# A hybrid decoder layer on one core: side work placed by modelled clocks, and an inverse that turns its blocks through DRAM

## The chip, the core and the metric

The kernel runs on one core of a Trainium2 chip. Its five engines (TensorE for matmuls, VectorE, ScalarE, GpSimd, and SyncE, which issues most DMAs) run side by side, each through its own queue in order. The metric is the device time of one execution in microseconds; the output must be the reference's.

## The reference

One decoder layer for 512 positions and a model width of 2048, all in float32. After an RMSNorm, one projection feeds three mixers: differential attention (4 heads, causal, ALiBi), sliding-window attention (8 query heads, window 128, sinks) and an RWKV-7 time mixing of 16 heads of 64 channels. Their outputs are concatenated, projected and added to the input; then come an RMSNorm, a SwiGLU feed-forward part of width 5632, and a last RMSNorm.

```python
def step(S, inp):                      # RWKV-7, per head, S is 64 x 64
    r_t, w_t, k_t, v_t, a_t, b_t = inp
    sa = jnp.einsum('bhvk,bhk->bhv', S, a_t)
    S = S * w_t[:, :, None, :] + sa[..., None] * b_t[:, :, None, :] + v_t[..., None] * k_t[:, :, None, :]
    return S, jnp.einsum('bhvk,bhk->bhv', S, r_t)

kk = kk / jnp.maximum(jnp.sqrt(jnp.sum(kk * kk, axis=-1, keepdims=True)), 1e-12)
y = wkv7_scan(r4, hs(decay), k4, v4, -kk, kk * a4)
```

## The kernel before

**Wide matmuls.** Every weight matrix is cut into items (`proj`, `wout_items`, `ffn_items`), and an item is 24 or 48 matmuls of 128 x 128 weights against 512 columns: weights and activations are split into a high and a low part (`weights`, L154), and three of the four products are summed. `sequence` runs the items one after another; while item n runs, item n+1's weights are loaded by SyncE into one of three `raw` buffers, cast by ScalarE (L169) and subtracted by VectorE (L170).

**Side work.** The mixers' other steps are generators in lanes. `dense_k` calls `pump` after every fourth wide matmul, and `pump` lets each lane go one step, to its next `yield`; so the order of TensorE, which is kept as written, is made by counting matmuls. `wait(n)` lets a lane pass n turns. `need(name)` pumps, with no wide matmul between, until a lane has finished.

**RWKV, by pairs of heads.** For each of eight pairs (`pair_items`) there are three items, `k`, `r`, `v`. `rates` makes decays: sigmoids, and one scan (L437) for each of eight chunks of 64 positions. `prep` makes the chunk matrices: `bt` (transposes), the products `gr` of both heads, masked by VectorE (L549) into `linv`, `zl` and `gr`, and `vt` and `bon`. `inverse` inverts the 64 x 64 unit triangles of eight chunks and two heads: the diagonal 32 x 32 blocks are copied together (L594 to L596), transposed on VectorE (L600), eliminated in 30 steps of two VectorE operations (L608, L609), transposed back twice (L617 `xtt`, L618 `xnn`), and the off-diagonal block comes from two groups of 16 matmuls, `pt` and `po`. `chain` then goes through the eight chunks: `z`, a copy on ScalarE, `u`, a copy, `S`, an update on VectorE (L678), and outputs `y`. `post` normalizes; `spill` writes the result to DRAM (`mix`).

**Attention.** `diff_head` and `swa_tile` work in blocks of 128 queries: `scores` (matmuls `sa`, `sb` and the softmax on VectorE and ScalarE), `turned` (transposes `wt`, `wtb`) and `values` (`oa`, `ob`), each a step of its own. Then the output projection `po` runs in two halves and, from 1050 us on, the feed-forward part.

Of the kernel before, what the change touches and what calls it, by code (L numbers as in the profile page):

```python
# [14 lines left out]
P = 128  # L15
# [34 lines left out]
for _name, _w in (  # L50
    ("ident", 128), ("onesbd", 128), ("ones", 128), ("centre", 128), ("mask", 128),
    ("eps", 1), ("gneps", 1),
):
    CST[_name] = _n
    _n += _w
# [3 lines left out]
def constants():  # L59
# [15 lines left out]
    put("gneps", np.full((P, 1), GN_EPS, np.float32))  # L75
    return c
# [10 lines left out]
class Kernel:  # L87
    def __init__(self, tc, ins, out, dbg=None, stop=None):
# [6 lines left out]
        self.lanes = [[], [], [], [], [], [], []]  # L95
        self.order = [self.lanes[j] for j in (2, 6, 5, 0, 1, 3, 4)]
        self.done = set()
        self.flags = set()
        self.count = 0
        self.quantum = 4  # L100
        self.delay = 150
# [21 lines left out]
    def tr(self, out, src):  # L123
        self.tc.keep_in_program_order(self.nc.tensor.transpose(out, src, self.cst("ident", P)))  # L124

    def pump(self):
# [9 lines left out]
    def wait(self, n):  # L139
        for _ in range(-(-n * 4 // self.quantum)):  # L140
            yield

    def need(self, name):
        for _ in range(10000):
            if name in self.done:
                return
            self.pump()
# [28 lines left out]
    def dense_k(self, ps, wts, rhs, k, n, m=P, cols=slice(0, T)):  # L176
        (his, los), (xh, xl) = wts, (x[:, cols] for x in rhs[k])
        for i, (w, x) in enumerate(((his[k], xh), (his[k], xl), (los[k], xh))):
            self.mm(ps[:m, :], w, x, start=(k == 0 and i == 0), stop=(k == n - 1 and i == 2))
            self.count += 1  # L180
            if self.count % self.quantum == 0:
                self.pump()
# [26 lines left out]
    def run(self):  # L209
        nc, tc = self.nc, self.tc  # L210
        with contextlib.ExitStack() as es:
            enter = es.enter_context
            self.cp = enter(tc.tile_pool(name="cp", bufs=1))
# [126 lines left out]
    def mixer_items(self, enter):  # L340
# [11 lines left out]
        f = rp.tile([P, T], F32, tag="r", name="f_wl")  # L352
# [8 lines left out]
        for j in range(2):  # L361
            def go(ps, j=j):
                f = rp.tile([P, T], F32, tag="r", name=f"f_gl{j}")
# [13 lines left out]
        for t in self.linv:  # L377
            nc.gpsimd.memset(t, 0.0)
        self.mix = [None] * 16
# [6 lines left out]
    def pair_items(self, hp):  # L386
# [5 lines left out]
        for j, n in ((1, "k"), (0, "r"), (2, "v")):  # L392
            def go(ps, n=n):
                if hp:
                    self.need(f"{n}{hp - 1}")
                f = self.rp.tile([P, T], F32, tag=n, name=f"{n}{hp}")
# [15 lines left out]
    def rates(self, hp):  # L412
# [4 lines left out]
        if not hp:  # L417
            yield from self.wait(16)
# [3 lines left out]
        g2 = rp.tile([P, 2, P], F32, tag="g2", name=f"g2_{hp}", bufs=3)  # L422
        nc.sync.dma_start(out=w2, in_=self.i["w2"][:, ch])
        nc.sync.dma_start(out=a2, in_=self.i["a2"][:, ch])
        nc.sync.dma_start(out=g2, in_=self.i["g2"][:, :, ch])
        q["g2"] = g2
# [5 lines left out]
        yield  # L432
        self.sigmoid(sg[:, :, 1:65], ps.rearrange("p (n c) -> p n c", c=C))
        yield from self.wait(2)
        cum = rp.tile([P, NCH, 65], F32, tag="kk", name=f"cum{hp}")
        for n in range(NCH):
            nc.vector.tensor_tensor_scan(out=cum[:, n], data0=self.cst("ones", 65), data1=sg[:, n], initial=0.0,  # L437
                                         op0=ALU.mult, op1=ALU.add)
        yield
        yield  # L440
# [5 lines left out]
        yield  # L446

        ps = self.pm.tile([P, T], F32, tag="m", name=f"pa{hp}")
        self.mm(ps, a2, self.al[:96, :], start=True, stop=True)
        yield  # L450
        a = rp.tile([P, T], F32, tag="a", name=f"a{hp}")
        self.sigmoid(a, ps, nbias=self.na0[:, hp:hp + 1])
        q["D"] = rp.tile([P, NCH], F32, tag="D", name=f"D{hp}", bufs=3)
        nc.vector.tensor_tensor(out=q["D"][:, 0:NCH - 1], in0=W[:, 0:NCH - 1, 64], in1=V[:, 1:NCH, 0], op=ALU.mult)
        q.update(W=W, V=V, a=a)

    def prep(self, hp):
# [8 lines left out]
        kk_g = self.col("k_k", hp)  # L466
        yield
        nc.scalar.activation(rn, k, AF.Square, scale=kk_g)
        yield from self.wait(1)
# [3 lines left out]
        yield  # L473
        nc.vector.tensor_scalar(out=kk, in0=ps, scalar1=1e-24, scalar2=None, op0=ALU.max)
        yield
        nc.scalar.activation(kk, kk, AF.Ln)
        nc.scalar.activation(kk, kk, AF.Exp, scale=-0.5)
        yield from self.wait(2)
        nc.vector.scalar_tensor_tensor(out=kk, in0=k, scalar=kk_g, in1=kk, op0=ALU.mult, op1=ALU.mult)
        yield  # L480
# [757 lines left out]
```

## Time and profile before

| | us |
|---|---|
| median of three runs | 2511.62 (2507.73 to 2515.35) |
| profiled execution | 2510.84 |
| its span, first to last instruction | 2509.0 |
| TensorE busy | 2445.0 (97%) |
| VectorE busy | 1277.2 (51%) |
| ScalarE busy | 835.3 (33%) |

Matmuls are pipelined and their recorded durations overlap, so the distance of two starts tells more than a duration, and 97% busy is not 97% of what TensorE could do. A wait is the idle time before an instruction together with what ended it. The granted clock is the share of TensorE's full clock, 2.4 GHz, that the chip let through; 0.50 is its lower level, 1.2 GHz.

### The profile page before, as it was taken

How to read it: one execution, taken by the hardware profiler on the slowest of the kernel's cores; microseconds unless marked ns; L12 is line 12 of the kernel's file. 1: busy time of each engine (PE TensorE's matmuls, PEld its weight loads, DVE VectorE, ACT ScalarE, POOL GpSimd, SP SyncE). 2: the span in 40 equal slices, each digit the busy share in tenths (PEclk: the TensorE clock that was granted, in tenths of full speed). 3: DMA queues.
4: the chain of work that ended last, by engine and by line, in shares of the span. 5: the costliest groups of instructions: out<-in, count | busy, mean ns of one | idle time of the engine just before them, and what ended most of it. 6: DMA issues, size and time to landing. Idle time of an engine off the chain costs nothing.

```text
span 2509.0 us, 30180 instructions
## 1 busy us (share of the span) xinstructions
PE 2445.0 (97%) x12072; PEld 1932.7 (77%) x12072; DVE 1277.2 (51%) x2201; ACT 835.3 (33%) x1439; POOL 92.4 (4%) x115
## 2 busy tenths in 40 slices
PE   8989999999999999999999999999999999999997
PEld 6766666666767678888888888888888888888887
DVE  6777788877454534434343433333343434343437
ACT  5544455553444523322222222222222222212224
POOL 3000000000000001200000000000000000000006
PEclk9989899999999999999999999999999999999999
DMA  5211111111322423323232323232322223232324
GB/s 180 75 51 59 57 59 59 59 55 59 100 78 89 145 93 126 101 93 98 95 100 94 101 93 101 93 101 93 101 94 99 96 98 97 96 99 95 101 93 135
DMA packets 76142, 232.65 MB, mean 93 GB/s; under 512 B 8282, under 2 KB 17122, under 8 KB 76002
## 3 DMA queue, kind: packets, MB, share of 16 engines
q1 hardware_dynamic: 71106, 224.04, 27.5%
q10 hardware_dynamic: 4896, 6.69, 0.8%
q8 instruction: 95, 1.56, 0.3%
q14 instruction: 45, 0.37, 0.0%
HBM read 222.30 MB, written 8.39 MB: 92 GB/s over the span
## 4 chain that ended last, share of the span: by engine, by line
PE 69%; DVE 1%; ACT 1%; issue 0%; POOL 0%; DVEq 0%; ACTq 0%; POOLq 0%
PE pg L121 19%; PE pu L121 19%; PE pd L121 18%; PE po L121 7%; PE pd_qb L121 1%; PE pd_va L121 1%; PE pd_qa L121 1%; PE pd_ka L121 1%; PE sb L121 0%; PE oa L121 0%; PE ob L121 0%; POOL acc L1053 0%; PE wtb L124 0%; PE sa L121 0%; DVE y L1151 0%
## 5 line engine op out<-in xcount | busy, mean ns | idle before, releaser
L121 PE MATMUL pd<-al,wh_wd 128*128 128x512 f32 (+1 forms) x768 | 285.3, 371 | 0.5 <-DVE al L1088 0.5
L121 PE MATMUL pd<-ah,wh_wd 128*128 128x512 f32 (+1 forms) x768 | 285.4, 372 | 0.4 <-DVE y L1107 0.4
L121 PE MATMUL pd<-ah,wl_wd 128*128 128x512 f32 (+1 forms) x768 | 285.2, 371 | 0.0
L121 PE MATMUL pu<-x1h,wh_wu 128*128 128x512 f32 x704 | 274.3, 390 | 0.0
L121 PE MATMUL pu<-x1h,wl_wu 128*128 128x512 f32 x704 | 273.9, 389 | 0.0
L121 PE MATMUL pu<-x1l,wh_wu 128*128 128x512 f32 x704 | 273.9, 389 | 0.0
L121 PE MATMUL pg<-x1h,wl_wg 128*128 128x512 f32 x704 | 273.9, 389 | 0.0
L121 PE MATMUL pg<-x1h,wh_wg 128*128 128x512 f32 x704 | 273.9, 389 | 0.0
L121 PE MATMUL pg<-x1l,wh_wg 128*128 128x512 f32 x704 | 273.9, 389 | 0.0
L1107 DVE TENSOR_TENSOR y<-y,pd 128x512 f32<-128x512 f32 (+1 forms) x192 | 122.7, 642 | 207.6 <-PE pd L121 207.4
L169 ACT CAST wh_wd<-raw_wd 128x1024 fp32r<-128x1024 f32 x96 | 101.0, 1052 | 356.8 <-PE pd L121 177.1
L169 ACT CAST wh_wu<-raw_wu 128x1024 fp32r<-128x1024 f32 x88 | 92.7, 1054 | 367.0 <-PE pu L121 144.7
L169 ACT CAST wh_wg<-raw_wg 128x1024 fp32r<-128x1024 f32 x88 | 92.7, 1054 | 362.5 <-PE pg L121 145.1
L170 DVE TENSOR_TENSOR wl_wg<-raw_wg,wh_wg 128x1024 fp32r<-128x1024 f32 x88 | 107.8, 1225 | 171.1 <-ACT wh_wg L169 171.1
L170 DVE TENSOR_TENSOR wl_wu<-raw_wu,wh_wu 128x1024 fp32r<-128x1024 f32 x88 | 107.8, 1225 | 133.4 <-ACT wh_wu L169 133.4
L121 PEld LDWEIGHTS pd<-al,wh_wd 128*128 128x128 f32 x768 | 144.7, 188 | 25.7 <-DVE al L1088 0.8
L121 PEld LDWEIGHTS pd<-ah,wh_wd 128*128 128x128 f32 x768 | 144.6, 188 | 25.6 <-issue 0.5
L121 PEld LDWEIGHTS pd<-ah,wl_wd 128*128 128x128 f32 x768 | 144.7, 188 | 25.0
L121 PEld LDWEIGHTS pu<-x1l,wh_wu 128*128 128x128 f32 x704 | 132.1, 188 | 27.7 <-issue 0.2
L121 PEld LDWEIGHTS pu<-x1h,wh_wu 128*128 128x128 f32 x704 | 132.1, 188 | 27.7 <-issue 0.2
L121 PEld LDWEIGHTS pg<-x1l,wh_wg 128*128 128x128 f32 x704 | 132.1, 188 | 27.5
L121 PEld LDWEIGHTS pg<-x1h,wh_wg 128*128 128x128 f32 x704 | 132.1, 188 | 27.4
(345 smaller groups left out, 4271.5 us busy)
## 6 DMA issues: line engine op xcount, KB each, us to landing
raw_wd<-in_w_down SPq DMA_DIRECT2D x96, 512.0 KB, 3.3
raw_wg<-in_w_gate SPq DMA_DIRECT2D x88, 512.0 KB, 3.7
raw_wu<-in_w_up SPq DMA_DIRECT2D x88, 512.0 KB, 3.7
raw_wo<-in_w_out SPq DMA_DIRECT2D x32, 512.0 KB, 3.2
raw_k<-in_w_in SPq DMA_DIRECT2D x16, 512.0 KB, 3.9
raw_r<-in_w_in SPq DMA_DIRECT2D x16, 512.0 KB, 3.7
raw_v<-in_w_in SPq DMA_DIRECT2D x16, 512.0 KB, 3.7
x<-in_xT SPq DMA_DIRECT2D x16, 256.0 KB, 5.2
```

The costliest lines, as they stand in the source:

```text
L121: self.tc.keep_in_program_order(self.nc.tensor.matmul(out, lhsT, rhs, start=start, stop=stop))
L169: nc.scalar.copy(out=hi[:, :kn * m], in_=s)
L170: nc.vector.tensor_tensor(out=lo[:, :kn * m], in0=s, in1=hi[:, :kn * m].bitcast(F32), op=ALU.subtract)
L1107: nc.vector.tensor_tensor(out=o, in0=o, in1=ps, op=ALU.add)
```

## The change

The generators no longer advance by counted matmuls but by a clock, `now`, to which `mm` and `tr` add a modelled duration. A callback, `charge`, adds up the work of VectorE and ScalarE in `free`. `pump` is called after every wide matmul; it lets a lane go on only when `now` has reached the lane's due time: the yielded number of microseconds later, or the modelled end of its last operation plus 0.3. The copies and updates of the chain are marked `urgent`, which puts them ahead on their engines. Many steps of `rates`, `prep` and attention are merged into one.

```diff
     def mm(self, out, lhsT, rhs, start=True, stop=True):
+        n, m = rhs.free_size(), lhsT.free_size()
+        if lhsT.dtype == F32R:
+            self.now += n / 2400 + 0.013
+        else:
+            self.now += 2 * max(n / 1200, m / 1200)
...
+    def charge(self, ins):
...
+        if eng == "DVE":
+            us = 0.14 + n * (0.0019 if ins.opcode == "StreamTranspose" or "Scan" in ins.opcode else 0.00104)
+        else:
+            us = 0.19 + n * 0.00085
+        self.free[eng] = max(self.free[eng], self.now + 0.2) + us
+        self.last = max(self.free[eng], self.last + us + 0.05)
...
     def pump(self):
+        moved = False
         for lane in self.order:
             if lane:
                 name, gen = lane[0]
+                if self.due.get(name, 0.0) > self.now:
+                    continue
+                moved = True
+                self.last = self.now
                 try:
-                    next(gen)
+                    wait = next(gen)
+                    self.due[name] = self.now + wait if wait else self.last + self.slack
...
     def need(self, name):
...
-            self.pump()
+            if not self.pump():
+                self.now = min(self.due[lane[0][0]] for lane in self.order if lane)
```

In `rates` one scan of 520 elements, with zeros that restart it, replaces eight of 65, and the two sigmoids stand together. In `prep` the floor under the squared norm moves from VectorE to ScalarE. `r` gets two buffers, `v` and `k` keep one. `inverse` becomes three parts: `prep` itself writes the four diagonal blocks to DRAM (`li`); `inverse` loads them with a block per partition (`x`), eliminates along columns, lets ScalarE make the transposed copy, and stores both (`xi`, `xj`); `join`, in a lane of its own, loads them back into `linv` and `xnn` and runs `pt` and `po`, now alternating between the heads at their own partitions.

```diff
+        for h, b, bl in blocks:
+            nc.sync.dma_start(out=d[h, b].rearrange("n s t -> s n t"), in_=L[bl, :, bl])
...
     def inverse(self, q):
...
+        yield 2.5
...
-        nc.vector.transpose(out=x, in_=nd.rearrange("p h n b t -> p t (h n b)"))
+        nc.sync.dma_start(out=x, in_=q["li"].rearrange("h b n s t -> (h b n) s t"))
+        yield 2.5
...
+            yield max(self.free["DVE"] - self.now - 1.0, 0.1)
-        nc.vector.transpose(out=xt.rearrange("p h n b t -> p t (h n b)"), in_=x)
-        nc.vector.transpose(out=xn.rearrange("p h n b s -> p s (h n b)"), in_=x.rearrange("p t s -> p s t"))
+        xt = rp.tile([32, 32, 32], F32, tag="i1", name="xtt")
+        nc.scalar.copy(out=xt[0:32].rearrange("p t s -> p s t"), in_=x)
...
+        nc.sync.dma_start(out=d.rearrange("h b n s t -> (h b n) s t"), in_=x)
+        nc.sync.dma_start(out=dt.rearrange("h b n t s -> (h b n) t s"), in_=xt)
...
+    def join(self, q):
...
+        yield 4.5
+        xn = rp.tile([P, NCH, 32], F32, tag="xn", name="xnn")
+        for h, b, bl in blocks:
+            nc.sync.dma_start(out=L[bl, :, bl], in_=d[h, b].rearrange("n s t -> s n t"))
+            if not b:
+                nc.sync.dma_start(out=xn[bl], in_=dt[h, b].rearrange("n t s -> t n s"))
+        yield 3
...
+        for n in range(NCH):
+            for h in range(2):
+                lo, hi = blocks[2 * h][2], blocks[2 * h + 1][2]
+                self.mm(ps[hi, n, :], L[lo, n, hi], xn[lo, n, :], start=True, stop=True)
```

In attention a step is now `turned(blk)`, `values(blk - 1)` and, where there is one, the next `scores`.

**TensorE at an inverse.** In the rows, the digit behind a name is the pair, and the last number tells buffers apart. Before, for pair 4:

```order
L121 MATMUL pd_k5_3000<-xh15_234,wl_k5_8_2817 128x512
L121 MATMUL pt_3123<-xnn_3108,n21_2649 32x32 x16
L121 MATMUL pd_r5_3155<-xh0_96,wh_r5_0_2990 128x512
L121 MATMUL pd_r5_3155<-xl0_97,wh_r5_0_2990 128x512
L121 MATMUL pd_r5_3155<-xh0_96,wl_r5_0_2991 128x512
L121 MATMUL pd_r5_3155<-xh1_106,wh_r5_0_2990 128x512
L121 MATMUL po_3166<-xtt_3107,pts_3140 32x32 x16
```

and in the change, after `pd_v5`, where pair 3's inverse falls into pair 4's products (`y3` between, repeated groups of `gr4` left out):

```order
L130 MATMUL pd_v5_3051<-xh15_234,wl_v5_8_2896 128x512
L130 MATMUL g2_3220<-sgl1_567,g2_2_2830 128x512
L130 MATMUL gr4_0_0_3226<-ar4_2844,bk4_2846 128x128
L130 MATMUL pt_3232<-xnn_3213,linv1_482 32x32 x16
L130 MATMUL po_3262<-linv1_482,pts_3249 32x32 x16
L130 MATMUL z3_0_3284<-uv3_2644,zl3_2499 64x64 x2
L130 MATMUL gr4_1_0_3289<-ar4_2844,bk4_2846 128x128
L130 MATMUL u3_0_3295<-zs3_0_3287,linv1_482 128x64
L130 MATMUL S3_0_3314<-uv3_2644,bkn3_2453 64x64 x2
L130 MATMUL vt4_3337<-cc_76,v4_2672 128x128 x4
L130 MATMUL u3_2_3378<-zs3_2_3362,linv1_482 128x64
L130 MATMUL pd_k6_3399<-xh0_96,wh_k6_0_3041 128x512
```

Between `pd_v5` and `pd_k6` stand 34 rows of small matmuls and no wide one; `pd_v7` is followed by the same piece for pairs 5 and 6. In the other pairs wide matmuls stand between `pt` and `po`.

**VectorE ahead of `bt4`.** `bt4` reads `bk4`. In the change VectorE has these rows between the chain's last update of pair 2 and the last piece of `bk4` (`xt` and `x` are the inverse of pair 3):

```order
L718 SCALAR_TENSOR_TENSOR uv2_2134<-S2_6_3122,D2_1425,uv2_2134 64x64 x2
L208 TENSOR_TENSOR wl_k6_0_3042<-raw_k6_0_3039,wh_k6_0_3041 128x1024
L518 SCALAR_TENSOR_TENSOR ar4_2844<-kk4_2839,W4_2711 128x8x64
L630 TENSOR_TENSOR x_2725<-x_2725,xt_2741 32x29x2
L521 TENSOR_TENSOR kk4_2839<-kk4_2839,a4_2701 128x512
L629 TENSOR_TENSOR xt_2741<-x_2725 32x30
L547 TENSOR_TENSOR ar4_2844<-r4_2526,W4_2711 128x8x64
L526 TENSOR_TENSOR bk4_2846<-kk4_2839,IW4_2712 64x8x64 x2
L527 TENSOR_TENSOR a4_2701<-a4_2701,k4_2392 128x512
L630 TENSOR_TENSOR x_2725<-x_2725,xt_2741 32x30
L531 TENSOR_TENSOR bk4_2846<-a4_2701,IW4_2712 64x8x64 x2
```

TensorE has 15 wide matmuls and four small groups between that update's `S` and `bt4`.

**SyncE's queue at the trip.** In the change, for pair 3:

```order
L203 DMA raw_r6_8_3393<-in_w_in 128x1024
L636 DMA xi3_3186<-x_2725 32x1024
L637 DMA xj3_3187<-xtt_3184 32x1024
L649 DMA linv1_482<-xi3_3186 32x8x32 x2
L651 DMA xnn_3213<-xj3_3187 32x8x32
L649 DMA linv1_482<-xi3_3186 32x8x32
L203 DMA raw_v6_0_3593<-in_w_in 128x1024
```

Two of the six loads back stand here as repetitions of rows shown; `raw` are the weight loads that stand before and behind.

## Rows read from the trace of the kernel before

**Rows 1.** the page, part 2: the granted TensorE clock in 40 slices, in tenths

```profile
PEclk9989899999999999999999999999999999999999
```

**Rows 2.** windows: length, busy us (count) by engine, clock, DMA share, GB/s

```profile
57.00:538.00 481.00, 453.06 (x2739) 323.89 (x2738) 377.84 (x859) 248.13 (x541) 3.27 (x32) 0.93 0.19 60
538.00:692.00 154.00, 148.78 (x934) 105.87 (x932) 101.59 (x226) 68.92 (x171) 0.00 (x0) 0.97 0.24 77
692.00:860.00 168.00, 160.33 (x794) 114.75 (x794) 82.44 (x252) 69.88 (x170) 0.00 (x0) 1.00 0.31 100
```

**Rows 3.** chain of waits, the first item of the feed-forward part: start, us, what

```profile
1050.22 10.89 PE pg L121 x48
```

**Rows 4.** waits: engine line, waited for: total us, times, longest

```profile
PE pt L121 <- DVE xnn L618: 23.5, 7, 5.9
```

**Rows 5.** timeline of TensorE at an inverse: start us, us, what, idle

```profile
360.24 0.40 PE L121 MATMUL pd_k<-xh,wl_k 128*128 128x512 f32 x1
362.72 1.78 PE L121 MATMUL pt<-xnn,n 32*32 32x32 f32 x32 [2.09 <-DVE xnn L618]
364.43 0.80 PE L121 MATMUL pd_r<-xh,wh_r 128*128 128x512 f32 x1
```

**Rows 6.** windows of the stretch behind that wait

```profile
363.00:373.00 10.00, 10.00 (x81) 7.56 (x78) 4.35 (x9) 2.62 (x6) 0.10 (x1) 0.50 0.17 54
```

**Rows 7.** timeline of TensorE, a group of gr and one of oa

```profile
358.78 0.71 PE L121 MATMUL gr<-ar,bk 64*128 64x128 f32 x8
359.42 0.50 PE L121 MATMUL pd_k<-xh,wl_k 128*128 128x512 f32 x1
359.76 0.40 PE L121 MATMUL pd_k<-xh,wh_k 128*128 128x512 f32 x1
...
696.74 1.13 PE L121 MATMUL oa<-wts,van 128*128 128x128 f32 x8
697.62 0.48 PE L121 MATMUL pd_qa<-xh,wl_qa 128*128 128x512 f32 x1
```

**Rows 8.** lines of TensorE, 75:905 us: busy, mean ns, idle before, releaser

```profile
L121 PE MATMUL oa<-wts,van 128*128 128x128 f32 x80 | 12.2, 283 | 3.3 <-ACT wts L837 3.3
L124 PE MATMUL wtb<-cc,pb 128*128 128x128 f32 x56 | 9.0, 277 | 4.4 <-DVE pb L919 4.4
```

**Rows 9.** lines of VectorE, 100 to 600 us, transpose and scan

```profile
L617 DVE STREAM_TRANSPOSE xtt<-x 32x1024 f32<-32x1024 f32 x7 | 13.6, 1942 | 0.1
L437 DVE TENSOR_TENSOR_SCAN cum<-cc,sg 128x65 f32<-128x65 f32 x56 | 11.2, 260 | 0.0
```

**Rows 10.** timeline of TensorE, a piece of chain without wide matmuls

```profile
580.18 0.33 PE L121 MATMUL u<-zs,linv 128*128 128x64 f32 x2
581.75 0.50 PE L121 MATMUL S<-uv,bkn 128*64 128x64 f32 x3 [1.24 <-ACT uv L668]
...
584.64 0.56 PE L121 MATMUL u<-zs,linv 128*128 128x64 f32 x2 [0.55 <-ACT zs L655]
```

**Rows 11.** lines of VectorE, 100 to 600 us, operations in the long stretches

```profile
L170 DVE TENSOR_TENSOR wl_r<-raw_r,wh_r 128x1024 fp32r<-128x1024 f32 x14 | 16.9, 1208 | 1.2 <-ACT wh_r L169 1.2
L549 DVE TENSOR_TENSOR linv<-gr,cc 64x256 f32<-64x256 f32 x30 | 12.5, 416 | 55.0 <-PE gr L121 54.6
L503 DVE TENSOR_TENSOR bk<-a,IW 64x512 f32<-64x512 f32 x14 | 9.5, 682 | 0.2
```

**Rows 12.** lines of ScalarE, 100 to 600 us, an operation on 1024 elements

```profile
L169 ACT CAST wh_r<-raw_r 128x1024 fp32r<-128x1024 f32 x14 | 14.7, 1047 | 25.5 <-PE pd_k L121 17.3 <-issue 8.1
```

**Rows 13.** DMA issues of the run: KB each, median us from issue to landing

```profile
mix<-ysq SPq DMA_DIRECT2D x8, 256.0 KB, 2.9
g<-in_g SPq DMA_DIRECT2D x8, 128.0 KB, 3.9
a<-in_a SPq DMA_DIRECT2D x8, 48.0 KB, 2.4
```

**Rows 14.** timeline of SyncE's queue: one load of g

```profile
210.00 0.56 SPq L425 DMA_DIRECT2D g<-in_g  x1
```

More of the change, by code (lines that the diff above doesn't have):

```diff
@@ L94, in __init__ @@
         self.stop = stop
-        self.lanes = [[], [], [], [], [], [], []]
-        self.order = [self.lanes[j] for j in (2, 6, 5, 0, 1, 3, 4)]
+        self.lanes = [[], [], [], [], [], [], [], []]
+        self.order = [self.lanes[j] for j in (2, 7, 6, 5, 0, 1, 3, 4)]
         self.done = set()
         self.flags = set()
-        self.count = 0
-        self.quantum = 4
-        self.delay = 150
+        self.now = 0.0
+        self.due = {}
+        self.free = {"DVE": 0.0, "Activation": 0.0}
+        self.last = 0.0
+        self.slack = 0.3
     def col(self, name, j=0, n=P):
@@ L137, in pump @@
                     self.done.add(name)
-    def wait(self, n):
-        for _ in range(-(-n * 4 // self.quantum)):
-            yield
+                self.last = self.now
+        return moved
     def need(self, name):
-        for _ in range(10000):
+        for _ in range(100000):
             if name in self.done:
                 return
-            self.pump()
+            if not self.pump():
+                self.now = min(self.due[lane[0][0]] for lane in self.order if lane)
         raise AssertionError(name)
@@ L417, in rates @@
         if not hp:
-            yield from self.wait(16)
+            yield 15
         ch = slice(hp * P, (hp + 1) * P)
@@ L615, in inverse @@
[L615 to L621 removed]
+            cl = x[:, j:j + 1, j + 1:32].to_broadcast([32, j, n])
@@ L622, in inverse @@
         for h in range(2):
-            for n in range(NCH):
-                self.mm(ps[:, h, n, :], n21[:, h, n, :], xn[:, h, n, 0, :], start=True, stop=True)
-        pt = rp.tile([32, 2, NCH, 32], F32, tag="pt", name="pts")
-        nc.scalar.copy(out=pt, in_=ps)
+            hi = blocks[2 * h + 1][2]
+            nc.scalar.copy(out=pt[hi], in_=ps[hi])
         yield
-        ps = self.pc.tile([32, 2, NCH, 32], F32, tag="c", name="po")
-        for h in range(2):
-            for n in range(NCH):
-                self.mm(ps[:, h, n, :], pt[:, h, n, :], xt[:, h, n, 1, :], start=True, stop=True)
@@ L632, in inverse @@
-        for h in range(2):
-            r0 = 64 * h
-            lo, hi = slice(r0, r0 + 32), slice(r0 + 32, r0 + 64)
-            nc.scalar.copy(out=L[lo, :, lo], in_=xt[:, h, :, 0, :])
-            nc.scalar.copy(out=L[hi, :, hi], in_=xt[:, h, :, 1, :])
-            nc.scalar.copy(out=L[lo, :, hi], in_=ps[:, h])
+        ps = self.pc.tile([P, NCH, 32], F32, tag="c", name="po")
+        for n in range(NCH):
+            for h in range(2):
+                lo, hi = blocks[2 * h][2], blocks[2 * h + 1][2]
+                self.mm(ps[lo, n, :], pt[hi, n, :], L[hi, n, hi], start=True, stop=True)
@@ L638, in inverse @@
+        for h in range(2):
+            lo, hi = blocks[2 * h][2], blocks[2 * h + 1][2]
+            nc.scalar.copy(out=L[lo, :, hi], in_=ps[lo])
         yield
@@ L654, in chain @@
             z = rp.tile([P, C], F32, tag="zs", name=f"zs{hp}_{n}", bufs=2)
-            nc.scalar.copy(out=z, in_=pz)
+            with self.urgent():
+                nc.scalar.copy(out=z, in_=pz)
+            back = self.last + self.slack - self.now
             if n:
@@ L663, in chain @@
                                              scale=q["D"][HALF[h], n:n + 1])
-            yield
+            yield back
             pu = self.pc.tile([P, C], F32, tag="c", name=f"u{hp}_{n}")
             self.mm(pu, L[:, n], z)
-            for h in range(2):
-                nc.scalar.copy(out=uv[HALF[h], n, h], in_=pu[HALF[h]])
+            with self.urgent():
+                for h in range(2):
+                    nc.scalar.copy(out=uv[HALF[h], n, h], in_=pu[HALF[h]])
             yield
@@ L856, in diff_head @@
             turned(blk)
-            yield
+            back = self.last + self.slack - self.now
+            if blk:
+                values(blk - 1)
             if blk < 2:
                 scores(blk + 2)
-                yield
-            values(blk)
-            yield
+            yield back
+        values(3)
         o = rp.tile([P, T], F32, tag="sq2", name=f"osq{h}")
```

174 lines of the change are left out of this document (83 added, 91 removed).

## The prediction

> **What bounds the kernel now.** I read the page's 40 slices first, then the windows by stage, TensorE's waits, its timeline around one of them, and the order in which the instructions stand. In the slices the clock falls below full speed only in the first quarter [rows 1]. The windows say which stages those are [rows 2]: the heads' projections (57 to 538 us, mean granted clock 0.93) and the end of the RWKV chains (538 to 692 us, 0.97); attention (692 to 860) runs at 1.00. From 1050 us on, an item of 48 wide matmuls takes 10.89 us [rows 3], 0.227 us a matmul, with nothing between. That part, 58% of the run, is untouched. TensorE is the path everywhere, so what the change is worth is its waits, its half-clock time and what it pays to switch between wide and small matmuls, before 1050 us.
>
> The largest wait is the triangular inverse's: `pt` waits 23.5 us in 7 waits, up to 5.9 us, for VectorE's second transpose `xnn` [rows 4]. One of them [rows 5]: the wide matmul before it starts at 360.24, `pt` at 362.72, its 32 records take 1.78 us, and the wide one after it takes 0.80 us instead of 0.40. The granted clock then stands at 0.50, the 1.2 GHz level, for ten microseconds [rows 6]. So a wait of 2.1 us costs about 2.1 + 5. Over the run the lost clock is 0.07 x 481 + 0.03 x 154 = 38 us of TensorE time [rows 2].
>
> **The change, part by part.** Its sum stands against the profiled execution, 2510.84 us (span 2509.0), 0.8 below the median of the three runs, 2511.62.
>
> *Gains.* (1) The waits of `pt` on the VectorE transposes go: -23.5. What is late next is the DRAM trip, priced below. (2) The half-clock time that follows them: 38 us less 2 for stretches that began elsewhere, -36. (3) Fewer switches. From the first wide matmul of `gl1` to the last attention matmul, the order has 372 blocks of small matmuls before and 314 after. A block's surcharge is read at the wide matmul behind it: 359.42 to 359.76 is 0.34 us where 0.227 is usual [rows 7], so 0.11 a block, 58 x 0.11 = -6. (4) `pt` and `po` alternate between the two heads, which now lie in different rows and columns of the array, as the halves of `gr` do: the eight records of `gr` are through in 0.64 us (358.78 to 359.42), while eight records of as many columns that fill the array, those of `oa`, take 0.88 (696.74 to 697.62) [rows 7]. `pt` took 1.78 at half clock [rows 5], so some 0.9 at full; side by side 0.45; two such groups in eight pairs: -7, bounds 0 and -14; I take -6.
>
> The Trainium skill, "TensorE: Matmul & The Clock Gate", part 3 on packing small matmuls, says that tiles of few rows in different row groups run at the same time; by that rule alone `pt` and `po` would halve, -7, and the trace agrees for `gr` [rows 7].
>
> (5) Attention's steps merged: `oa` waits 3.3 us and `wtb` 4.4 us for the softmax and its copies [rows 8]. With `turned`, `values` and the next `scores` in one step, a step comes back only when the modelled engines are through; I take half: -4. VectorE loses three transposes of about 1.95 us and eight scans of 0.26 us a pair [rows 9] for one scan of the same 520 elements. None of it is on TensorE's path except through (1), and VectorE stays below TensorE (378 of 481 us busy [rows 2]), so it is priced at nothing; were it late, the chain's `uv` updates would be late with it, which the losses below contain. ScalarE exchanges small copies for one copy of 1024 elements: nothing, off the path. Gains: -75.5.
>
> *Losses.* (a) Two stretches without cover. In pairs 4 and 6 the order puts the whole of `gr`, `pt`, `po`, `vt`, `bon` and three chain steps between the last matmul of `pd_v5` (`pd_v7`) and the next wide one, since `v` has one buffer and `need` pumps on until it is free; in the order before, no stretch without a wide matmul is longer than six small groups. The trace has one short uncovered piece of chain: u at 580.18, S 581.75, and after z the next u at 584.64: three links, 1.49 us each [rows 10]. Seven links lie in the stretch: 10.4 us. Ahead of them stand `g`, the first `gr`, `pt` and `po`; the second `gr` waits for six maskings of 0.42 us [rows 11], because `gr` has two PSUM buffers. I put the stretch at 14 us: 10.4 and some 3.5 ahead of it. TensorE works 7.9 of it, an estimate: four groups of `gr` at 0.64 [rows 7], 0.9 for `pt` and `po`, about 0.2 for each of twelve chain groups, 2 for `g`, `vt` and `bon`. Idle 6.1; bounds 3 (half links, since the chain's copies now go first on their engines) and 10. Before it `bt4` stands where VectorE still has, behind the chain's update `uv`, one weight subtraction of 1.21 and eight operations of 0.68 [rows 11]: 8 us against 5 of cover on TensorE (15 wide matmuls and four small groups), 2.5 to 3 us of wait. And the clock: 4.5, from the 5 above, some of it falling on waiting. Per stretch 6.1 + 2.5 + 4.5 = 13.1, twice: +26. (b) In pair 7 all of `gr` stands together: 2.5 us for the maskings, 1 for its operands, 4 for the clock: +7.5.
>
> (c) The DRAM trip, which no row of before shows. From VectorE's last step to `pt`: ScalarE's copy of 1024 elements, 1.05 us [rows 12]; the store from issue to landing, 2.4 as `a` or 2.9 as `mix` [rows 13]; then the loads, which SP issues in line at 0.56 each as for `g`, also of 256 pieces [rows 14], of which two or three stand before the last one that `pt` needs, 1.1 to 1.7; and its landing, 2.4 as `a`, up to 3.9 as `g` [rows 13]. Together 7.0, at the upper end 9.6. The generators reserve 4.5 + 3 from a point at most a microsecond ahead of VectorE. I take the lower end, since `a` is nearest in size (48 KB against 32) and the engines are little used (DMA share 0.19 [rows 2]): waits of 0 to 1.5 us in six pairs, clock included 1.5 each: +9. SP's queue gains 13 transfers a pair, at 0.56 some 7 us of issuing in a pair of 60 (eight pairs in 481 us [rows 2]). The weight loads behind them stand an item (11 us and more) ahead of use, so this is priced at nothing; without that lead each blocked load would show as a wait of `wh`. VectorE also waits in line for `x` from DRAM; four issues and two landings, 7 us, stand against one chain step and four large operations, so no wait or one of 1 us, held in (c).
>
> Losses +42.5. Sum -75.5 + 42.5 = -33: 2510.84 - 33 = 2478.
>
> **The rivals.** *Slower: the trip takes longer than reserved.* If it lasts 9.6 us and more, `pt` waits 2 to 3.5 us in all eight pairs, each wait brings the half clock back, 8 x (3 + 5) = 64 in place of the 9 of (c): 2478 + 55 = 2533. It decides from about 2 us over the reserve, 8 x (2.1 + 5) - 9 = 48 [rows 5, 6], that is 2526. For it: 128-byte pieces occur nowhere in the trace, and four stores must land before one load. Against it: `a` with its short pieces lands in 2.4 us and the DMA engines are four fifths idle here.
>
> The Trainium skill, "VectorE: DVE Perf Modes", in its rules for kernel authors, calls VectorE's own transpose the fastest for 32 x 32 blocks, and "DMA: Bandwidth & Descriptors" warns in its rules of plain copies that rearrange: by these the inverse is later in itself. The rows agree that the transposes are short; whether anybody waits is the order's matter.
>
> *The cover holds everywhere.* If the links in the two stretches take half, no half clock follows and the trip is within its reserve, losses fall to 2 x 5 + 4 = 14: 2510.84 - 75.5 + 14 = 2449. For it: the change lets the chain's copies overtake on ScalarE and VectorE, and the 1.49 us links contain ScalarE's other copies. Against: the order shows the stretches.
>
> *Nothing left.* If the modelled clocks run wrong by a microsecond, waits of about one microsecond return at many of the 314 blocks; some 30 of them take back the 33 us: 2511. The clocks charge a small group nothing for its switch, which makes TensorE later than modelled; that speaks against waits, and for a few per cent more cover.
>
> **How the numbers follow.** The sum as computed has 0.46, with 2462 to 2497 of its own (the bounds of (a), (c) and (4)). The full cover has 0.23, around 2449; nothing left 0.17, 2497 to 2520, of which a third is still faster; slower by the trip 0.14, 2520 to 2534. A measurement here tells 0.3%, 7.5 us, from no change. Faster: 0.46 + 0.23 + 0.06 = 0.75. Slower: 0.14 + 0.01 = 0.15. Same: 0.10. The range 2447 to 2513 leaves out the slow case and a little of the full cover.
>
> **What would show it.** Right: the waits of TensorE have no `pt` on VectorE any more, or a fraction on a DMA; the clock from 57 to 692 us has two or three dips instead of eight; two stretches of about 14 us without wide matmuls; `pt` with 32 records in under 1 us; the step at 1050 us comes at about 1018. Wrong: `pt` waiting 2 us and more on `xnn` loads in every pair with the half clock behind it; weight casts waiting on SP; or a start of the feed-forward part later than 1043.

## The result and the profile after

The changed kernel takes 2480.46 us (median of four runs, 2478.83 to 2481.82) against 2510.68 of the kernel before (four runs, 2507.73 to 2515.35): ratio 0.9878, 95% interval 0.9860 to 0.9895. That is 30 us or 1.2% faster; forecast were 33 us and 2478. The profiled execution took 2481.82 us (span 2480.0). All of the gain lies ahead of the feed-forward part. In the chain of waits its first item now starts at 1021 us and takes what it took [rows 3]; columns are start, us, what:

```profile
1021.21 10.89 PE pg L130 x48
```

The windows of [rows 2] after the change, and as a fourth row the long stretch behind `pd_v` of pair 5 (columns as there: length, busy us by engine, granted clock, DMA share, GB/s):

```profile
57.00:538.00 481.00, 457.76 (x2846) 328.78 (x2846) 348.91 (x788) 247.09 (x512) 3.23 (x32) 0.96 0.25 73
538.00:692.00 154.00, 146.69 (x940) 104.62 (x939) 94.22 (x239) 68.83 (x163) 0.00 (x0) 0.99 0.29 89
692.00:860.00 168.00, 161.36 (x803) 120.54 (x802) 85.25 (x240) 70.07 (x164) 0.00 (x0) 1.00 0.33 110
370.60:384.30 13.70, 12.56 (x65) 9.25 (x65) 4.83 (x13) 5.08 (x17) 0.00 (x0) 0.50 0.13 34
```

By the first two rows 0.04 x 481 + 0.01 x 154 = 21 us of clock are still lost, 38 before. The fourth row is where a third of it goes: 13.7 us at the 1.2 GHz level, with TensorE busy in 12.6 of them. So the recorded waits are a small part of it; how much the lower clock lengthens it is looked at with the run warm below.

The waits of TensorE, 46 to 1050 us (what waited, for what: us in total, times, longest):

```profile
PE bt L134 <- DVE bk L531: 19.6, 8, 3.6
PE wt L134 <- DVE pa L868: 6.2, 6, 1.9
PE gr L130 <- DVE gr L574: 5.7, 6, 2.4
PE wt L134 <- DVE st L861: 1.2, 1, 1.2
PE z L130 <- ACT uv L599: 0.9, 1, 0.9
PE z L130 <- DMA linv<-xi: 0.9, 1, 0.9
```

`pt`, 23.5 us before [rows 4], is gone from the list. The 0.9 us put down to a load of `linv` is a wait of the decay product `z<-wl,w`, which doesn't read `linv`:

```profile
311.30 1.12 PE L130 MATMUL z<-wl,w 97*128 97x512 f32 x2 [0.88 <-DMA linv<-xi]
```

Two pairs later the same product waits as long with ScalarE named, so nothing on TensorE is seen to wait for the trip. In the first place stands a wait that was 3.1 us before: `bt`, the transposes of `bk`, now waits for VectorE in all eight pairs. One of them, in TensorE's and VectorE's timelines (start, us, engine line, what, idle before):

```profile
279.79 0.39 PE L130 MATMUL pd_r<-xl,wh_r 128*128 128x512 f32 x1
282.40 1.11 PE L134 MATMUL bt<-cc,bk 128*128 128x128 f32 x4 [2.22 <-DVE bk L531]
283.16 0.78 PE L130 MATMUL pd_r<-xh,wl_r 128*128 128x512 f32 x1
...
276.79 0.69 DVE L518 SCALAR_TENSOR_TENSOR ar<-kk,W 128x512 f32<-128x512 f32 x1 [0.42 <-PE y L130]
277.40 0.39 DVE L629 TENSOR_TENSOR xt<-x 32x240 f32<-32x240 f32 x1
277.72 0.67 DVE L521 TENSOR_TENSOR kk<-kk,a 128x512 f32<-128x512 f32 x1
278.32 0.39 DVE L630 TENSOR_TENSOR x<-x,xt 32x240 f32<-32x240 f32 x1
278.64 1.37 DVE L526 TENSOR_TENSOR bk<-kk,IW 64x512 f32<-64x512 f32 x2
280.04 0.69 DVE L527 TENSOR_TENSOR a<-a,k 128x512 f32<-128x512 f32 x1
280.65 0.39 DVE L629 TENSOR_TENSOR xt<-x 32x238 f32<-32x238 f32 x1
280.97 1.37 DVE L531 TENSOR_TENSOR bk<-a,IW 64x512 f32<-64x512 f32 x2
```

VectorE isn't idle: three operations of an inverse (L629, L630) lie between those of `prep` and, by the distances of the starts (0.32 us each), make `bk` about 1 us later than it would be alone. Behind the wait the wide multiplication takes 0.78 us in place of 0.39: such a wait comes with a dip to the half clock too, in five of the eight pairs.

**An account for all kernels.** In the table, "start" is the start of the feed-forward part in the profiled execution; "half" the time between 46 us and it at the 1.2 GHz level, added up from the trace's clock records; "idle" all gaps between TensorE's instructions there; "rest" is start - idle - half/2. (Idle time within a stretch at half clock counts twice, so the rest comes out low where stretches hold waits: 14.3 us of it in count_trip, 15.5 in v_two and 12.4 in rates_early, 2 to 7 in the others. Counted once, the rest is 970.7 before, 969.7 in count_trip and 963.0 in the change; in the runs below that keep the clocks and add no work to TensorE it is 959.4 to 966.1, and 967.0 in h_outer.)

| kernel | median us | ratio to before (95%) | start | half | idle | rest |
|---|---|---|---|---|---|---|
| before | 2510.7 | | 1050.1 | 81.9 | 41.6 | 967.5 |
| the change | 2480.5 | 0.9878 (0.9860, 0.9895) | 1021.0 | 44.4 | 37.2 | 961.7 |
| clock_dve | 2518.1 | 1.0024 (1.0014, 1.0033) | 1056.9 | 102.4 | 45.5 | 960.2 |
| count_trip | 2492.5 | 0.9926 (0.9914, 0.9939) | 1033.6 | 58.0 | 42.0 | 962.5 |
| bt_late | 2485.4 | 0.9896 (0.9882, 0.9909) | 1024.6 | 58.0 | 35.4 | 960.2 |
| tight | 2504.2 | 0.9968 (0.9956, 0.9981) | 1043.4 | 58.0 | 51.9 | 962.5 |
| res | 2492.2 | 0.9927 (0.9914, 0.9939) | 1030.9 | 58.0 | 43.4 | 958.5 |
| v_two | 2506.9 | 0.9984 (0.9975, 0.9993) | 1050.0 | 81.9 | 55.6 | 953.4 |
| rates_early | 2522.8 | 1.0057 (1.0043, 1.0071) | 1062.1 | 109.2 | 54.2 | 953.2 |
| h_outer | 2484.2 | 0.9893 (0.9880, 0.9907) | 1023.4 | 44.4 | 35.4 | 965.8 |
| att_apart | 2483.2 | 0.9889 (0.9875, 0.9902) | 1022.7 | 51.2 | 36.3 | 960.8 |
| scans8 | 2482.1 | 0.9884 (0.9870, 0.9897) | 1020.8 | 51.2 | 37.3 | 957.9 |
| warm | 2477.7 | 0.9865 (0.9850, 0.9880) | 1018.9 | 34.1 | 31.6 | 970.2 |
| warm_bt | 2476.2 | 0.9862 (0.9846, 0.9879) | 1015.5 | 23.9 | 28.0 | 975.5 |

The change's 29 us at the start are 18.8 of half clock (81.9 - 44.4, halved), 4.4 of idle time and 5.8 of rest; with that idle time counted once, 16.9, 4.4 and 7.7.

### The profile page after: what moved, and what is told of

It is laid out like the page before. It is cut to its first block, busy times and chain, and to the rows that moved or that the text cites. A ratio compares the mean times of both kernels' runs of the same rounds, so it can differ in the third digit from the quotient of the medians.

```text
span 2480.0 us, 30228 instructions
## 1 busy us (share of the span) xinstructions
PE 2419.3 (98%) x12072; PEld 1921.0 (77%) x12072; DVE 1230.6 (50%) x2113; ACT 824.2 (33%) x1383; POOL 93.0 (4%) x117
## 4 chain that ended last, share of the span: by engine, by line
PE 91%; DVE 6%; ACT 1%; issue 1%; DMA 1%; POOL 0%; SPq 0%; DVEq 0%; ACTq 0%; POOLq 0%
PE pg L130 19%; PE pu L130 19%; PE pd L130 19%; PE po L130 7%; PE pd_k L130 4%; PE pd_r L130 3%; PE pd_v L130 2%; PE pd_va L130 2%; PE pd_qb L130 2%; PE pd_qa L130 2%; PE pd_ka L130 1%; PE z L130 1%; PE pd_l L130 1%; PE y L130 1%; PE gr L130 1%
```

## The experiments

**Order and trip apart.** clock_dve keeps the order made from clocks and takes the trip out; count_trip keeps the old order by counts and puts the trip in.

```diff
 clock_dve, in inverse(), against the change
-        nc.sync.dma_start(out=x, in_=q["li"].rearrange("h b n s t -> (h b n) s t"))
+        nc.vector.transpose(out=x, in_=nd.rearrange("p h n b t -> p t (h n b)"))
...
+        nc.vector.transpose(out=xt.rearrange("p h n b t -> p t (h n b)"), in_=x)
+        nc.vector.transpose(out=xn.rearrange("p h n b s -> p s (h n b)"), in_=x.rearrange("p t s -> p s t"))
 count_trip, in inverse() and join(), against the change (the order is that of before)
-        yield 2.5
+        yield from self.wait(3)
...
-        yield 4.5
+        yield from self.wait(5)
...
-        yield 3
+        yield from self.wait(4)
```

> The changed kernel with VectorE's three transposes and ScalarE's copies of before in the place of the trip through DRAM, in the clocks' order (the products still in a step of their own, due when VectorE's modelled work is done). Theory (order and trip each bring a part: the clocks place the products, the trip only takes 8 x 3 x 1.95 us of transposes off VectorE): 2488 to 2500 us, pt waits on VectorE under 8 us in all, and a stretch of 18 small multiplications without a wide one in five pairs. Rival A (all of the gain is the order): 2478 to 2484. Rival B (all of it is the trip): 2505 or more, with pt waits near 23 us again.

> The kernel of before, ordered by counts, with only the inverse replaced by the trip through DRAM (its two reserves and the lead of the first load as 3, 3, 5 and 4 counts of four wide multiplications). Theory: the 23.5 us of pt waits and most of the half clock behind them go, but two stretches of 28 small multiplications in pairs 4 and 6 come: 2483 to 2497 us. Rival A (all of the gain of the change is the order): 2505 to 2515, with pt or linv waiting on DMA or VectorE instead. Rival B (all of it is the trip): 2476 to 2483.

The edits part the two not quite cleanly: the alternation of `pt` and `po`, worth some 4 us by h_outer below, goes with the trip and is missing in clock_dve, which also has three buffers for the small weights (`w2`) in place of four.

Of clock_dve both the theory and its rivals fell (the time lies in rival B's open interval, but the waits of `pt` that were to cause it are not there): the order without the trip makes the kernel 0.24% slower than before. It does place `pt` well (2.3 us of waits), and still loses, to the clock. Its windows 57 to 538 and 538 to 692 us, and the half clock at one of five stretches with 18 to 20 groups of small multiplications and no wide one (this stretch ends at 263.8 us, the dip outlasts it):

```profile
57.00:538.00 481.00, 451.41 (x2659) 322.07 (x2658) 368.06 (x762) 242.47 (x518) 3.23 (x32) 0.91 0.19 61
538.00:692.00 154.00, 147.45 (x969) 104.79 (x967) 102.77 (x237) 71.08 (x183) 0.00 (x0) 0.94 0.20 64
256.30:270.00 13.70, 13.30 (x45) 7.63 (x43) 8.91 (x22) 8.58 (x23) 0.10 (x1) 0.50 0.03 10
```

One account fits, though no run shows it by itself: the loop of the pairs has no reserve. A pair's `rates` begins when the `prep` before it ends, and `prep` shares VectorE with the inverse. By the kernel's own clocks the generators then stand 57 us in all until a buffer is free, 30 us in the change. The 27 us between are about what three transposes take over five pairs (5 x 3 x 1.95 = 29 [rows 9]). Whatever is added to this loop would come out as a stretch that nothing wide covers.

count_trip lands in its theory's interval: the trip, with the alternation, brings 0.74%. Its counts keep too short a lead for the trip, and `pt` waits for the load instead:

```profile
PE pt L121 <- DMA xnn<-xj: 14.7, 6, 6.4
PE po L121 <- ACT pts L641: 8.5, 5, 3.2
```

So the parts are not additive: trip with the old order -0.74%, order without the trip +0.24%, both -1.22%. What the clocks add to the trip is that they keep its length free. Whether a longer lead by counts would do the same was not tried.

**How long the trip takes.** tight and res cut the modelled reserves; tight the slack too.

```diff
-        yield 4.5
+        yield 3.5
-        yield 3
+        yield 2
 tight alone:
-        self.slack = 0.3
+        self.slack = 0.1
```

> The changed kernel with the modelled reserves cut: 3.5 and 2 us for the trip's two ends (4.5 and 3), and 0.1 us of slack after a step (0.3). The order then has uncovered stretches of 18 to 20 small multiplications in pairs 4 and 6 (34 now). Theory (stretches at half clock cost, and the reserves are longer than needed): 2470 to 2477 us, with two long dips of the clock of under 8 us. Rival (the reserves are needed): z, u, S or pt wait for ScalarE, VectorE or DMA, 10 to 25 us more, 2488 to 2505.

> The changed kernel with only the reserves of the trip cut, 3.5 and 2 us for 4.5 and 3 (the slack of 0.3 us stays); the stretches in pairs 4 and 6 keep their 34 small multiplications. It parts the two edits of the run with both. Theory (it was the slack that cost there, the trip has room): 2478 to 2484 us, pt waits under 3 us. Rival (the reserves are what the trip takes, the prediction's 9 us): pt or z wait for DMA by 1 to 2 us in most pairs, with dips behind them, 2488 to 2505.

The times lie in the rivals' intervals, the signs only in part: in res one wait of `pt` is 4.8 us long and one 1.8, the other four 0.4 or less, and in tight it is `bt` that waits more. res costs 0.49% against the change; TensorE's waits in it, second row:

```profile
PE pt L130 <- DMA xnn<-xj: 7.6, 6, 4.8
```

In SyncE's queue, VectorE's and ScalarE's timelines of that 4.8 us wait the trip can be followed step by step:

```profile
358.37 0.20 DVE L630 TENSOR_TENSOR x<-x,xt 32x30 f32<-32x30 f32 x1
360.92 1.98 ACT L633 COPY xtt<-x 32x1024 f32<-32x1024 f32 x1
362.92 0.33 SPq L637 DMA_DIRECT2D xj<-xtt  x1
363.29 1.50 SPq L649 DMA_DIRECT2D linv<-xi  x3
365.38 0.80 SPq L651 DMA_DIRECT2D xnn<-xj  x2
```

`pt` starts at 367.1: 8.5 us after VectorE's last step, 2.4 of them ScalarE's other work ahead of the copy. In count_trip the same way took 6.5 us (356.56 to 363.1). The reserve of 4.5 + 3 is right to a microsecond. tight costs 0.9% in another way: `bt` waits 27.9 us, `pt` for no DMA at all; the steps come too close for VectorE.

**The wait of bt.** bt_late makes `bt` due 2.5 us later.

```diff
-        yield
+        yield max(self.last - self.now, 0.0) + 2.8
```

> The changed kernel with the transposes bt of each pair due 2.5 us later than they are now. Theory (the 19.6 us that bt waits for bk on VectorE, in eight pairs, and the six 3.4 us stretches of half clock behind them, are now the largest loss): bt waits under 3 us in all, half clock under 30 us, 2453 to 2468 us. Rival (the later bt only hands the wait on to gr, the inverse and the two uncovered stretches): 2474 to 2486, with the waits of gr or z grown by 10 us or more.

The rival's time holds: `bt` waits 8.1 us in place of 19.6, two of the five short dips at `bt` are left, and the kernel isn't faster (0.9896, the change 0.9878). Its sign holds less well: the waits of `gr` and `z` grow by some 3 us, not by 10. What is won comes back mainly in pairs 4 and 6, where `pt` now waits for the trip (5.0 us) and the stretch at half clock is 20.5 us long, twice:

```profile
363.90:384.40 20.50, 19.09 (x144) 13.90 (x144) 7.38 (x18) 7.83 (x24) 0.10 (x1) 0.50 0.22 56
497.00:517.50 20.50, 18.74 (x144) 13.66 (x145) 7.67 (x19) 7.29 (x23) 0.00 (x0) 0.50 0.21 56
```

**The uncovered stretches.** v_two gives `v` a second buffer; rates_early gives `a` one and lets `rates` begin when the pair before has its `r`. To make room, both also put the loaded inverse and the products of `pt` into one tile and give `w2` three buffers in place of four (not shown in the lines below).

```diff
 v_two
-                b = 2 if n == "r" else 1
+                b = 2 if n in "rv" else 1
 rates_early
-        while hp and f"prep{hp - 1}" not in self.done:
+        while hp and f"r{hp - 1}" not in self.done:
```

> The changed kernel with two buffers for v (the 2 KB come from sharing one tile between the loaded inverse and the products, and from three instead of four w2 buffers). The order has no stretch behind v4 and v6 any more, but one of 29 small multiplications behind r5's projection, 22 behind r7's and 13 before. Theory (pairs lag because their chain of steps takes longer than their projections; a buffer only moves the place): 2475 to 2486 us, half clock 40 to 60 us. Rival (the prediction's account, the single buffer of v makes the two stretches, 13 us each): 2455 to 2468.

> The changed kernel with a second buffer for a, so that a pair's rates begin when the pair before has its r, and not when that pair's prep has ended. The order then has 15 and 16 small multiplications behind v4 and v5, none behind v6, and 41 behind v7's projection (16 now). Theory (a step taken out of the pairs' loop shortens it, but the lag comes out at pair 7): 2474 to 2484 us. Rival A (the pairs' loop is shortened for good): 2460 to 2472, half clock under 35 us. Rival B (41 small multiplications in one stretch): 2486 or more, with a dip of the clock of 17 us or more at pair 7.

They are 1.1% and 1.8% slower than the change. v_two is worse than its theory and its rival had it; the time of rates_early lies in its rival B's open interval ("2486 or more"), though the longest dip at pair 7 is 13.7 us and not 17. The two stretches behind `pd_v` grew shorter or went, as the orders said, and longer ones came elsewhere: 23.3 us between two projections in v_two (381.79 to 405.10) and 25.6 in rates_early (576.40 to 602.04), 18.3 and 17.0 in the change:

```profile
381.79:405.10 23.31, 18.10 (x148) 11.60 (x147) 12.06 (x34) 13.39 (x34) 0.00 (x0) 0.62 0.14 40
576.40:602.04 25.64, 18.22 (x175) 12.90 (x175) 14.81 (x27) 11.68 (x32) 0.00 (x0) 0.70 0.18 49
```

A reading that fits, and that neither run shows by itself: with more buffers the projections run further ahead, and when the pairs' loop has at last to be waited for, more small work stands in one piece. rates_early loses by two other things as well. The decay product `z<-wl,w`, now right behind `gr`, waits 1.4 to 1.9 us in seven pairs, 11.0 in all (both lines together), and most of these waits have a dip beside them:

```profile
PE z L130 <- issue: 8.0, 5, 1.9
PE z L130 <- DVE gr L574: 3.0, 2, 1.5
```

And its longest dip is no piece of small work: it begins behind a wait of `pt` for the trip (2.6 and 0.8 us), holds one of those waits, and 23 wide multiplications run in it at half clock. TensorE is busy for 32.6 of its 37.5 us:

```profile
450.00:487.50 37.50, 32.62 (x184) 21.78 (x185) 15.47 (x43) 15.10 (x40) 0.10 (x1) 0.50 0.11 28
```

So `v`'s single buffer sets where the stretches are; with a second one they are elsewhere.

warm puts wide multiplications into the stretches, on operands that are there and into a result that nobody reads:

```diff
             if not self.pump():
-                self.now = min(self.due[lane[0][0]] for lane in self.order if lane)
+                idle = min(self.due[lane[0][0]] for lane in self.order if lane) - self.now
+                self.now += idle
+                self.owed += idle if name[0] in "krv" else 0.0
+                if self.owed > 0.7:
+                    self.owed -= 0.7
+                    w = self.xr[0][0]
+                    ps = self.pc.tile([P, T], F32, tag="c", name="warm")
+                    self.mm(ps, w[:, 0:P], w)
```

> The changed kernel with 32 wide multiplications more (128x512, operands that are there anyway, a result that nobody reads), put where the order has no projection to set between the small ones: one for each 0.7 us that the model idles while it waits for a buffer of k, r or v; 11 in pair 4's stretch and 11 in pair 6's. They add 32 x 0.226 = 7.2 us of work. Theory (a stretch costs what it runs at half clock, 6.9 and 5.1 us in pairs 4 and 6, and the small multiplications in it are held up by VectorE at their sides anyway): both long dips gone, half clock 18 to 28 us, 2472 to 2481 us. Rival A (wide ones this far apart do not bring the clock back): dips as now, 2486 to 2490. Rival B (the clock is back, but the stretch takes as long, since its length is VectorE's and ScalarE's): 2479 to 2483, with waits of z, u, S or vt for them where there are none now.

> The later bt (2.5 us) and the wide multiplications that nobody reads in one kernel; the later bt gives the model more to idle, and with one for each 0.5 us there are 51 of them (11.5 us). Theory (the later bt alone won its waits and lost them to two dips of 20.5 us in pairs 4 and 6; wide work in these stretches keeps the clock): both dips under 8 us, half clock under 28 us, 2470 to 2477 us. Rival (what the later bt hands on is a lateness of VectorE and of the trip, not the clock): waits of pt, gr, z or S as in the run with the later bt, and 2479 to 2488 us.

warm lands in its theory's interval (half clock 34, not 18 to 28: the two long dips shrank to 6.8 each). 7.2 us of work more, and the time is 2477.7. Pair 4's piece of chain, from its first `z` to the third `u`, in the change and then in warm:

```profile
369.46 0.33 PE L130 MATMUL z<-uv,zl 64*64 64x64 f32 x4
382.64 0.53 PE L130 MATMUL u<-zs,linv 128*128 128x64 f32 x2
```

```profile
372.34 0.33 PE L131 MATMUL z<-uv,zl 64*64 64x64 f32 x4
383.14 0.33 PE L131 MATMUL u<-zs,linv 128*128 128x64 f32 x2
```

It takes 10.8 us in place of 13.2, with five wide multiplications more in it: most of what the halved dip (13.7 to 6.8) should give. So the stretch is long in good part because its small multiplications run at half speed. warm_bt, with `bt` late and 51 such multiplications at 0.5 us, has no long dip left, and 2476.2 us. Its windows around pairs 4 and 6:

```profile
360.00:390.00 30.00, 28.43 (x241) 18.64 (x241) 17.18 (x43) 17.88 (x46) 0.10 (x1) 0.99 0.22 51
490.00:520.00 30.00, 29.37 (x257) 20.02 (x256) 20.89 (x52) 17.52 (x47) 0.00 (x0) 0.99 0.19 46
```

Clock and idle time give back 10 + 9 us against the change, the added work takes 11.5 and some 2 more. It starts the feed-forward part 3.4 us ahead of warm with 4.3 us more to do, and `pt` waits 0.8 us where it waited 5.0 with the late `bt` alone; what that run had won was lost mainly to the clock. The medians are 3 and 4 us below the change's; the intervals overlap, so against the change these two are better by the medians and by their traces, and not by the interval.

**Smaller parts.** h_outer runs `pt` and `po` one head after the other; att_apart takes attention's merged steps apart; scans8 puts eight scans back.

```diff
 h_outer, twice
-        for n in range(NCH):
-            for h in range(2):
+        for h in range(2):
+            for n in range(NCH):
 att_apart, in diff_head (in swa_tile likewise)
-            back = self.last + self.slack - self.now
-            if blk:
-                values(blk - 1)
+            yield
             if blk < 2:
                 scores(blk + 2)
-            yield back
-        values(3)
+                yield
+            values(blk)
+            yield
 scans8
-            nc.vector.tensor_tensor_scan(out=cum.rearrange("p n c -> p (n c)"), data0=self.keep,
+        for n in range(NCH):
+            nc.vector.tensor_tensor_scan(out=cum[:, n], data0=self.cst("ones", 65), data1=sg[:, n], initial=0.0,
```

> The changed kernel with the loops of pt and po turned round: the 16 records of one head, then the 16 of the other, as before the change; nothing else moves. Theory now (a record of 32 rows starts every 27 ns at full clock whichever head it is of, half of what it took at half clock before): pt and po stay at 0.88 us for 32 records, 2479 to 2482 us. Rival (the prediction's term 4: records of the two heads run beside each other): pt and po 0.4 us longer each in eight pairs, 2486 to 2488.

> The changed kernel with attention's steps apart again as before the change (scores, transposes and values each with a step of their own), in the clocks' order. Theory now (the merge only exchanged waits: wt on VectorE 6.2 us for oa and wtb 7.7 us): 2476 to 2484 us, with oa and wtb waits back and wt waits gone. Rival A (the prediction's term 5): 2483 to 2486. Rival B (more steps than the projections can hold, so that the last of them come without cover ahead of the output's projection): 2490 to 2505, with half clock at 900 to 1020 us.

> The changed kernel with eight scans of 65 a pair again in the place of the one of 520: 7 x 8 more instructions on VectorE, and the modelled clocks count them. Theory (VectorE is not what rates waits for, but the pairs' loop has no reserve, so that 1.5 us more in it per pair comes out partly): 2482 to 2492 us. Rival (hidden altogether): 2479 to 2482.

In h_outer it was the "theory now" that was wrong: it read `pt` in pair 4, which takes 0.89 us there because its records pause for 0.22 us behind the second one. In pair 3 the timelines show, of h_outer and then of the change:

```profile
314.86 1.09 PE L130 MATMUL pt<-xnn,linv 32*32 32x32 f32 x32
315.88 0.50 PE L130 MATMUL pd_k<-xh,wl_k 128*128 128x512 f32 x1
```

```profile
316.68 0.69 PE L130 MATMUL pt<-xnn,linv 32*32 32x32 f32 x32
317.30 0.50 PE L130 MATMUL pd_k<-xh,wl_k 128*128 128x512 f32 x1
```

From `pt` to the next wide one 1.02 us and 0.62: 0.40 for a group. Three of the change's sixteen groups have the pause and win 0.13, so 5.6 us in all by the rows; the rest in the table rises by 4.1 and the median by 3.8, although the time's intervals overlap. att_apart (+2.7 us) and scans8 (+1.7) can't be told from the change by their times; a dip of 6.8 us at 930 us, which the change doesn't have, is 3.4 of att_apart's. In att_apart `wt` waits 0.8 us, and `wtb` (3.2) and `oa` (2.5) wait again.

## Why the prediction was right, term by term

The time came out 2.5 us from the forecast; the mechanism (waits of `pt`, the clock behind them, two new stretches) is what the traces show, and several terms were mis-sized in ways that cancel. That they cancel is luck. One of the prediction's own signs failed: between 57 and 692 us the clock has eight dips, not two or three (nine before), though six of the eight last only 3.4 us.

- **(1) the waits of `pt`, -23.5:** right, no wait of `pt` is left in the list.
- **(2) the clock, -36, with the 4.5 twice in (a) and the 4 in (b), -23 net:** measured -18.8. Before's half clock cost 41 us by the records and not 38; nearly all of it left its places (the dip at one `bt` of before, at 138 us, has its counterpart in the change). The dips in pairs 4 and 6 cost 6.9 and 5.1 where 4.5 each was put. Beyond them five dips of 3.4 us stand at waits of `bt`, 8.5 us lost, of which the prediction had only the 2 for stretches that began elsewhere.
- **(3) fewer switches, -6:** open. Counted between projections, the order of count_trip has 350 blocks of small multiplications and the change 300, both with `pt` and `po` alternating. The rest in the table differs by 0.8 us, but count_trip's is low by idle time counted twice; counted once it differs by 6.7, where 50 x 0.11 is 5.5. The runs with the clocks' order scatter over 6.7 us among themselves, so neither -6 nor nothing is shown.
- **(4) `pt` and `po` side by side, -6:** right: 5.6 us in the rows, 4.1 in the rest. The Trainium skill's "TensorE: Matmul & The Clock Gate", part 3, would have them halve; 1.02 to 0.62 us with the wide one's own interval in it agrees.
- **(5) attention, -4:** mis-sized by the waits. `oa`, `wtb` and `wt` waited 8.8 us before; `wt`, `p_van` and `sa` wait 8.6 now. The wait moved to the transposes `wt`, which wait for the softmax. att_apart's time doesn't exclude a gain of a few microseconds.
- **(a) two uncovered stretches, +26:** they came where they were said to, in pair 4 with 18.3 us from the first small multiplication (364.60) to the next `pd_k` (382.93) for 14 forecast. The make-up was wrong: idle 1.5 us, not 6.1, since `gr`, `vt` and `bon` stand between the chain's links and fill them (the links are longer, not shorter: seven from 369.46 to 382.64, 1.9 us each for 1.49). With 6.1 us lost to half clock inside them, the 18.3 us leave some 10.7 of work where 7.9 was put: 2 us was put for `g`, `vt` and `bon`, and `g` alone takes 1.8. `bt4` waits 2.3 as said, although the 8 us of VectorE ahead of it add up to 6.65 as listed and reach 7.8 only with the inverse's three operations; clock 6.9. Together 10.7 in pair 4, some 9 in pair 6, for 13.1 each. "Since `v` has one buffer" gives the place and not the whole cause: v_two has two, and half clock and idle time are larger.
- **(b) pair 7, +7.5:** `gr` waits 2.4 us there once, with one dip of 3.4: about 4.
- **(c) the trip, +9:** its length of 7.0 us was well put (6.5 and 8.5 seen), though ScalarE's transposed copy takes 2.0 us and not 1.05 [rows 12]. What failed is "waits of 0 to 1.5 us in six pairs": the reserve covers it, and nothing is seen to wait for it.
- **Not in the sum:** `bt` in every pair. The prediction priced the lateness of VectorE only in pairs 4 and 6 (2.5 each); 19.6 us are 11.5 more than those and the 3.1 of before.

So (a), (b) and (c) were some 18 us too dear and (2) 5 too small; (5) and the waits of `bt` with their clock were 24 us too favourable. That puts the time 1 us above the sum if (3) held, and 7 if it brought nothing; the profiled execution came out 4 above it. The forecast is closer than its terms.

Of the rivals, "slower by the trip" has its mechanism in res: with 2 us less of reserve over a third of the gain goes. In the change itself it did not occur. "VectorE: DVE Perf Modes" of the Trainium skill, which has VectorE's own transpose as the fastest, is right of the transposes (1.94 us [rows 9], the trip 6.5) and still leads the wrong way here: clock_dve follows it and loses 1.5% to the change, some 4 us of that by the missing alternation. The account above would say why (VectorE's time counts in the pairs' loop, the trip's does not), but it is argued and not shown.

## What to carry to other kernels

Where TensorE is the path and its clock falls when wide work is missing, an order is judged by its waits and by its stretches without wide multiplications together: tight has shorter stretches than the change (10.0 and 13.7 us) and loses by waits. In the two tries here more buffers moved the longest stretch and lengthened it. A detour that is longer but leaves the loaded engine alone can win, if the order keeps just its length free; a wait that is mended by delaying its step comes back at the next place where the loop is waited for, so mend the loop or cover the place. Before a stretch is mended by hand, a few wide multiplications that nobody reads tell cheaply what the clock in it is worth.

## What was not expected of the hardware

- A wait of 2 to 3.6 us at `bt` had a dip of the granted clock of 3.4 us beside it in five of eight pairs, and in the other three (2.2 to 2.3 us) none. The longest dip, 37.5 us in rates_early, began behind waits of 3.4 us in all and went on with TensorE busy for 32.6 of them and 23 wide multiplications in it, seven of these with nothing between. Eleven wide multiplications within the 18 us stretch halved its dip (13.7 to 6.8).
- The records of multiplications of 32 rows and 32 columns started every 16 ns on average when these alternate between the two heads' partitions (0.50 us from first to 32nd record) and every 29 ns when they don't (0.90, h_outer).
- ScalarE's copy of 32 x 1024 with a transposed output took 1.98 us, a cast of 128 x 1024 in order 1.05.
- DMAs of 32 KB in pieces of 128 bytes (`li`, `linv`, `xnn`) landed in 1.6 to 3.0 us, no later than `g` of before with 128 KB in 3.9 [rows 13]. The trip's issues in the change (KB each, median us from issue to landing; `x`, `xi` and `xj` go in whole rows):

```profile
li<-linv SPq DMA_DIRECT2D x32, 32.0 KB, 1.6
x<-li SPq DMA_DIRECT2D x8, 128.0 KB, 2.4
xi<-x SPq DMA_DIRECT2D x8, 128.0 KB, 1.9
xj<-xtt SPq DMA_DIRECT2D x8, 128.0 KB, 2.1
linv<-xi SPq DMA_DIRECT2D x32, 32.0 KB, 2.0
xnn<-xj SPq DMA_DIRECT2D x16, 32.0 KB, 3.0
```
